# The low part of the attention keys, padded with zero rows to the full height of the matrix array

## The chip, the cores and the metric

One core of a Trainium2 chip runs the kernel. The metric is the device time of one execution in microseconds. Below, PE is TensorE's matrix products, PEld its loads of stationary operands, DVE is VectorE, ACT ScalarE, POOL GpSimd, and SP the engine that issues most DMAs.

## The reference

A single encoder block over 1024 tokens of 1024 channels. A normalised input h goes through one wide projection. Branch A is a bidirectional mLSTM, branch B a neighbourhood attention over a 16 by 64 grid of tokens with 8 heads of 64 channels; the branches are gated, projected, merged and added to the input. The part that the change touches is the score product of branch B:

```
sc = einsum('bhcid,bhacjd->bhciaj', q_blk, k_blk) * scale     # d = 64
sc = where(col_mask, sc + bias, NEG)
p  = softmax(sc)
o  = einsum('bhcin,bhcnd->bhcid', p, v_blk)
```

Everything is float32.

## The kernel before

Every float32 operand x of a matrix product is split in two: hi, which is x rounded to the reduced float32 form of TensorE (float32r), and lo = x - hi. A product is made of hi by hi, hi by lo and lo by hi.

The program runs in stages: the front (normalisation, h transposed, the first projection), then branch B, then the projection of B, then branch A, then the output. The instructions of PE stand in an order written out by hand: `weave` emits a filler, which is a string of dense projections (`dense_cm`, tiles `dps`, 128 rows by 512 columns each), and between its parts the pieces of chains, each piece not before a lag, counted in columns of matrix work, has passed. The other engines' instructions are ordered by the framework's scheduler, except in the front.

In branch B the filler is the projections to v and z, to the merge gates, and to q and k of the next pair of heads; the chain `na_chain` does the attention, one piece after three dense products. The heads are taken in four pairs, the two heads of a pair in the two halves of the 128 partitions. For a pair there are 16 blocks, a block being 128 queries of one head; in all 64. A block consists of

- `na_scores`: two products into one PSUM tile `sps`, then the row maximum (DVE, L766), the exponential (ACT, L768) and the division (DVE, L770, L771), giving `pt`;
- `na_weights`, after the scores of the next block: two or three transposes of `pt` on PE into `tps`, copied to `ptr` as hi and lo;
- `na_values`, two blocks later: products of `ptr` with one stationary tile `vb`, in pairs, into `ops`.

In `na_qk` the PSUM banks of the q and k projection are emptied into three tiles of a pair. `qA[:, hh]` holds a head's 64 rows of hi of q in one half of the partitions and of lo in the other. `kB[:, hh]` holds hi of k in both halves (the second half is a DMA copy). So one product of 128 rows, `qA` by `kB`, gives hi by hi plus lo by hi. `kl` holds lo of k, both heads of a pair in one tile of 128 partitions and 1024 columns, a head in its own half. The second product takes the 64 rows of hi from `qA` and the 64 rows of that head from `kl`. Both products have 384 columns for the inner six blocks of a head and 256 for the two at the edge: 48 and 16 in all.

Of the kernel before, what the change touches and what calls it, by code (L numbers as in the profile page):

```python
# [13 lines left out]
F32R = mybir.dt.float32r  # L14
# [27 lines left out]
def f32(ap):  # L42
    return ap.bitcast(F32)


class Build:
# [3 lines left out]

    # ---------------------------------------------------------------- helpers
    def pool(self, name, bufs=1, **kw):
        return self.tc.tile_pool(name=name, bufs=bufs, reuse_waits="tile", **kw)

    def load_w(self, src, c0, kt0, nk, ncols):
        """Rows kt0*128.. of src, columns as (start, count) parts, to a hi and a lo part."""
        return self.split_w(self.load_raw(src, c0, kt0, nk, ncols), nk, ncols)
# [30 lines left out]
    def weave(self, fill):  # L88
        """Emits fill, whose parts need nothing but loads and splits, and between its parts
        those of the chains, each not before its lag (us of matrix work) has passed.  # L90
        A generator yields a lag, or the name of a flag to wait for."""
        held, alive = None, True
        while True:
            late = None
            for e in self.chains:
                if isinstance(e[0], str):
                    if e[0] not in self.flags:
                        continue
                    e[0] = self.pe
                if late is None or e[0] < late[0]:  # L100
                    late = e
            if held in self.flags:
                held = None
            free = alive and held is None
            if late is not None and (late[0] <= self.pe or not free):
                try:
                    v = next(late[1])
                    late[0] = v if isinstance(v, str) else self.pe + v
                except StopIteration:
                    self.chains.remove(late)  # L110
            elif free:
                try:
                    v = next(fill)
                    held = v if isinstance(v, str) else None
                except StopIteration:
                    alive = False
            else:
                assert not self.chains and not alive, (held, [e[0] for e in self.chains])
                return

    def mm3(self, out, lh, rh, start, stop):
        """(hi + lo).T @ (hi + lo) without lo.T @ lo."""
        self.mm(out, lh[0], rh[0], start, False)
        self.mm(out, lh[0], rh[1], False, False)
        self.mm(out, lh[1], rh[0], False, stop)

    def dense_cm_steps(self, cols, weights, rhs, got):
        """Channel-major: 256 columns against rhs tiles; four banks [ch tile][t half].
        Yields before each half of each k."""
        ncols = sum(n for _, n in cols)  # L130
# [17 lines left out]
    def dense_cm(self, src, cols, rhs, evac, nk=NK, nst=NST):  # L148
        """As dense_cm_steps, each bank in turn over a part's nst rows of tiles."""
        ncols = sum(n for _, n in cols)  # L150
# [16 lines left out]
    def dense_tm(self, src, cols, lhs, evac):  # L167
        """Token-major: 256 columns; bank b holds token tiles 2b and 2b+1."""
        banks = [self.psd.tile([P, 2, 256], F32, name="dps", tag="d") for _ in range(4)]
# [18 lines left out]

    # ---------------------------------------------------------------- constants
    def setup(self):  # L190
# [46 lines left out]

    # ---------------------------------------------------------------- adaLN RMSNorm, h^T
    def front(self, cols):
        """h^T, with the first projection (256 columns) and that of the gates following its tiles."""  # L240
        nc, io = self.nc, self.io
# [229 lines left out]

    # ---------------------------------------------------------------- gate rows of the mLSTM
    def gate_weights(self, raw):
        """Gate columns of w_in as [k, 128]: i forward at 0, i backward at 32, f at 64 and 96;
        of each the four hi parts, then the lo ones."""
        nc, gp = self.nc, self.gwp
# [8 lines left out]
    def gate_rows(self, ps):  # L485
        """Pre-activations, a row per direction and head; the backward ones in reversed time.
        Those of the lo parts of the weights lie four rows on."""
        nc = self.nc
# [82 lines left out]
    def out_gate(self, fp):  # L571
        """Half the residual gate as a row in DRAM."""
        nc, io = self.nc, self.io
# [30 lines left out]

    # ---------------------------------------------------------------- neighbourhood attention
    def na(self, first, gps, ps0, ps1, fill):
        nc, io = self.nc, self.io
        self.yb = [self.ybp.tile([P, T], F32, name=f"yb{p}") for p in range(4)]
        with self.pool("na") as np_:
# [5 lines left out]
            self.ptr = [np_.tile([P, 8, 3, P], F32R, name=f"ptr{a}") for a in range(2)]  # L615
            self.na_pair = {}
            for a in range(2):
                for h in range(2):
                    self.na_qk(0, a, h, first[a])
# [21 lines left out]
    def na_qk(self, pair, a, h, banks):  # L641
        """q as [hi; lo] of each head, k as hi twice and lo; tokens by blocks of 8 columns."""
        nc, np_ = self.nc, self.np_
        if a == 0 and h == 0:
            qA = np_.tile([P, 2, T], F32R, name="qA")
            kB = np_.tile([P, 2, T], F32R, name="kB")
            kl = np_.tile([P, T], F32R, name="kl")
            self.na_pair[pair] = {"qk": (qA, kB, kl)}
        qA, kB, kl = self.na_pair[pair]["qk"]
        src = banks[h].rearrange("p (r c j) -> p r c j", r=8, c=8)  # L650
        for hh in range(2):
            own, oth = slice(hh * 64, hh * 64 + 64), slice(64 - hh * 64, 128 - hh * 64)
            q, k, l = [t.rearrange("p (c r j) -> p r c j", c=8, r=16)[:, h * 8:h * 8 + 8] for t in (qA[:, hh], kB[:, hh], kl)]
            if a == 0:
# [29 lines left out]
    def na_chain(self):  # L684
        """Blocks of 8 columns of queries of each head: scores, then weights, then values."""
        n = 4 * 16
# [48 lines left out]
    def na_head(self, pair, hh):  # L735
        """Tables of 8 * bias + mask, rows of keys beside those of queries."""
        nc, io, np_ = self.nc, self.io, self.np_
# [14 lines left out]
    def na_scores(self, hd, b):  # L752
        nc, np_, hh = self.nc, self.np_, hd["hh"]
        qA, kB, kl = self.na_pair[hd["pair"]]["qk"]
        rows = slice(hh * 64, hh * 64 + 64)
        kbs = [k for k in (b - 1, b, b + 1) if 0 <= k < 8]
# [5 lines left out]
        self.mm(sv, qA[:, hh, qs], kB[:, hh, ks], True, False)  # L762
        self.mm(sv, qA[rows, hh, qs], kl[rows, ks], False, True)
        p_ = np_.tile([P, 384], F32, name="pt", bufs=2)[:, 0:n]
# [51 lines left out]

    # ---------------------------------------------------------------- merge gates, branch B projection
    def gmerge(self, br, g):
        """tanh((g + b) / 2) of 256 channels of branch br, to DRAM."""
        nc, io = self.nc, self.io  # L820
# [32 lines left out]

    # ---------------------------------------------------------------- mLSTM
    def conv(self, mp, banks, ct, out):
        """3-tap convolution over tokens and x * (1 + tanh(x / 2)), which is 2 silu(x)."""
        nc = self.nc
# [70 lines left out]
    def state_step(self, C, kw, v, c, dt, dec, first):  # L928
        """C (fp32, [d, 2, 258]) updated with chunk c."""
        nc = self.nc  # L930
# [104 lines left out]
    def ml_scores(self, mp, c, qh, kh, hd, Pm):  # L1035
        """S^T of chunk c, times the decays of both directions, as hi and lo blocks."""
        nc = self.nc
# [28 lines left out]
    def gated_out(self, mp, hd):  # L1066
        """Output gate, per-head RMSNorm, SiLU gate path; y^T to DRAM."""
        nc, io = self.nc, self.io
# [62 lines left out]
    def branch_a(self):  # L1131
        """Branch A and its projection, whose first products run beside the last of y."""
        nc, io = self.nc, self.io
# [13 lines left out]

    # ---------------------------------------------------------------- merge, output projection, final norm
    def ya_tile(self, k):
# [9 lines left out]
    def proj_a(self, ms, fs):  # L1159
        """Merged branches, in bands of 256 channels; k 6 and 7 hold the last head."""  # L1160
        nc, io = self.nc, self.io
# [65 lines left out]
    def out_tile(self, fp, tt, mhi, mlo, who, wlo, grep, fg):  # L1227
        """128 tokens of the output projection, residual and final RMSNorm."""
        nc, io = self.nc, self.io
# [92 lines left out]
def build(arrays):  # L1322
    nc = bacc.Bacc("TRN2", target_bir_lowering=False, num_devices=1)
    io = {n: nc.dram_tensor("in_" + n, v.shape, mybir.dt.from_np(v.dtype), kind="ExternalInput").ap() for n, v in arrays.items()}
# [11 lines left out]
```

## Time and profile before

| what | value |
|---|---|
| median of 3 runs | 1332.75 us (1330.42 to 1333.08) |
| span of the profiled execution, first to last instruction | 1329.1 us |
| what the median has beyond that span | 3.65 us |
| PE busy | 1305.2 us, 98% of the span |
| DVE, ACT, POOL busy | 49%, 43%, 31% |

The profile is of one execution. The page gives its span and not what lies around it, so the median stands beside the span with 3.65 us more. A busy PE isn't a PE at its peak: matrix products are pipelined, each record is longer than the time from its start to the start of the next, and ends of records are modelled. So the starts are read here, not the ends. The stretch in which the attention blocks lie goes from 86 to 415 us.

### The profile page before, as it was taken

What the parts mean: (1) busy time and instruction counts of PE and PEld (TensorE: products, weight loads), DVE (VectorE), ACT (ScalarE), POOL (GpSimd) and SP (SyncE); (2) the same over time, 40 slices, a digit from 0 to 9 for tenths busy, and PEclk for the clock granted to TensorE, in tenths of its full rate; (3) what the DMA queues carried; (4) which work ended last, traced back from release to release, by engine and by line L of the source; (5) the groups of instructions that cost most, each with busy time, mean ns of one, the idle gap of its engine ahead of it and who ended that gap; (6) DMA issues with size and microseconds to landing.
All of it is one profiled execution on the core that took longest, in us unless ns stands there. A gap on an engine that the chain in (4) does not pass through costs nothing.

```text
span 1329.1 us, 19861 instructions
## 1 busy us (share of the span) xinstructions
PE 1305.2 (98%) x7560; PEld 1127.5 (85%) x7560; DVE 651.8 (49%) x1381; ACT 566.7 (43%) x1191; POOL 418.5 (31%) x381
## 2 busy tenths in 40 slices
PE   8799999999999899999999999999999999999997
PEld 8677777777777688988999989999989989888886
DVE  6944536435345441347626654555625641533533
ACT  6564434334444412336424553364434543423322
POOL 2634434335324423222212222222222212153332
PEclk9999999999999999999999999999999999999999
DMA  9633222222223364112111121112111122446432
GB/s 291 155 88 92 72 61 72 76 56 72 69 66 95 107 208 119 48 41 72 46 42 44 45 73 48 41 44 77 40 40 45 44 80 86 160 136 196 160 101 89
DMA packets 106187, 116.24 MB, mean 87 GB/s; under 512 B 9724, under 2 KB 86012, under 8 KB 106092
## 3 DMA queue, kind: packets, MB, share of 16 engines
q1 hardware_dynamic: 97352, 102.69, 27.1%
q10 hardware_dynamic: 8740, 12.29, 2.7%
q8 instruction: 59, 0.97, 0.3%
q14 instruction: 36, 0.29, 0.1%
HBM read 92.48 MB, written 20.08 MB: 85 GB/s over the span
## 4 chain that ended last, share of the span: by engine, by line
PE 91%; DMA 3%; DVE 2%; SPq 1%; ACT 1%; issue 1%; POOL 0%; ACTq 0%; POOLq 0%; DVEq 0%
PE dps L79 67%; PE ops L79 8%; PE ips L79 5%; PE sps L79 4%; PE cps L79 3%; PE tps L83 1%; PE wps L83 1%; DMA t_d<-gtmp 1%; SPq L251 1%; DMA wor<-in_w_out 1%; DMA wa<-in_w_ada 1%; PE kps L83 0%; PE ytp L83 0%; DVE acc L280 0%; PE gaps L79 0%
## 5 line engine op out<-in xcount | busy, mean ns | idle before, releaser
L74 POOL TENSOR_TENSOR wlo<-wraw,whi 128x512 fp32r<-128x512 f32 x168 | 227.0, 1351 | 585.9 <-ACT whi L73 576.0
L79 PE MATMUL dps<-hhi,whi 128*128 128x512 f32 x768 | 318.7, 415 | 1.0 <-ACT gtmp L827 0.6
L79 PE MATMUL dps<-hhi,wlo 128*128 128x512 f32 x768 | 302.6, 394 | 0.0
L79 PE MATMUL dps<-hlo,whi 128*128 128x512 f32 x768 | 298.8, 392 | 0.0
L79 PE MATMUL dps<-whi,hhi 128*128 128x256 f32 x768 | 217.1, 283 | 0.0
L79 PE MATMUL dps<-wlo,hhi 128*128 128x256 f32 x768 | 217.1, 283 | 0.0
L79 PE MATMUL dps<-whi,hlo 128*128 128x256 f32 x768 | 217.0, 283 | 0.0
L73 ACT ACTIVATE whi<-wraw 128x512 fp32r<-128x512 f32 x168 | 105.6, 629 | 228.6 <-PE dps L79 186.5
L79 PEld LDWEIGHTS dps<-hhi,whi 128*128 128x128 f32 x768 | 145.3, 189 | 32.2 <-issue 10.6
L79 PEld LDWEIGHTS dps<-hhi,wlo 128*128 128x128 f32 x768 | 145.2, 189 | 32.3
L79 PEld LDWEIGHTS dps<-hlo,whi 128*128 128x128 f32 x768 | 145.3, 189 | 18.6 <-DVE hlo L342 0.4
L79 PEld LDWEIGHTS dps<-wlo,hhi 128*128 128x128 f32 x768 | 146.9, 191 | 0.2
L79 PEld LDWEIGHTS dps<-whi,hhi 128*128 128x128 f32 x768 | 146.9, 191 | 0.2
L79 PEld LDWEIGHTS dps<-whi,hlo 128*128 128x128 f32 x768 | 146.9, 191 | 0.0
L79 PE MATMUL dps<-ya,whi 128*128 128x512 f32 x256 | 79.3, 391 | 0.0
L768 ACT ACTIVATE pt<-pt,mx 128x384 f32<-128x384 f32 (+1 forms) x64 | 37.7, 589 | 94.6 <-DVE mx L766 94.2
L1052 POOL TENSOR_TENSOR dg<-negm,mmask 128x256 f32<-128x256 f32 x32 | 25.0, 781 | 98.7 <-issue 28.9
L79 PEld LDWEIGHTS dps<-ya,whi 128*128 128x128 f32 x256 | 47.6, 188 | 9.7 <-DVE t0r L1182 0.2
L79 PE MATMUL ops<-woh,mlo 128*128 128x512 f32 (+1 forms) x136 | 51.3, 377 | 0.0
L79 PE MATMUL ops<-wol,mhi 128*128 128x512 f32 (+1 forms) x136 | 51.2, 377 | 0.0
L79 PE MATMUL ops<-woh,mhi 128*128 128x512 f32 (+1 forms) x136 | 51.2, 377 | 0.0
L79 PE MATMUL dps<-ya,wlo 128*128 128x512 f32 x128 | 49.9, 389 | 0.0
(265 smaller groups left out, 2359.1 us busy)
## 6 DMA issues: line engine op xcount, KB each, us to landing
wraw<-in_w_in SPq DMA_DIRECT2D x112, 256.0 KB
wa<-in_w_ada SPq DMA_DIRECT2D x16, 512.0 KB
wraw<-in_w_in SPq DMA_DIRECT2D x64, 128.0 KB
t_d<-gtmp ACTq DMA_DIRECT2D x32, 256.0 KB
xt<-in_x SPq DMA_DIRECT2D x8, 512.0 KB
wag<-in_w_ada SPq DMA_DIRECT2D x16, 256.0 KB
t1r<-t_d SPq DMA_DIRECT2D x8, 512.0 KB
mp_d<-t1r SPq DMA_DIRECT2D x16, 256.0 KB
```

Source lines behind the costliest of these rows:

```text
L73: nc.scalar.activation(hi, raw, AF.Copy)
L74: nc.gpsimd.tensor_tensor(lo, raw, f32(hi), op=ALU.subtract)
L79: self.nc.tensor.matmul(out, lhsT=lhsT, rhs=rhs, start=start, stop=stop, skip_group_check=True)
L83: self.nc.tensor.transpose(out, src, ident)
L251: nc.sync.dma_start(wa[:, :, s, :], wv[:, :, s, k, :])
L768: nc.scalar.activation(p_, p_, AF.Exp, bias=mx, scale=-1.0, accum_out=sm)
L1052: nc.gpsimd.tensor_tensor(dg, negm.rearrange("p (a b) -> p a b", a=2), mk, op=ALU.add)
```

## The change

`kl` becomes one tile of 128 partitions, two heads and 1024 columns, made once for all pairs. For each head the half of the partitions that isn't its own is set to zero once, by two GpSimd memsets of 64 rows by 1024 columns each, ahead of the first `na_qk`. The head's lo of k goes to its own half as before. The second score product takes all 128 rows of `qA[:, hh]` and of `kl[:, hh]`: the rows of lo of q meet zeros. It has the same stationary operand as the first one. In the build, the memory set aside per partition for dynamic DMA descriptors is given as 1024 bytes. All else in the diff is comments and docstrings that became blank lines.

```diff
+            self.kl = np_.tile([P, 2, T], F32R, name="kl")
+            for hh in range(2):
+                nc.gpsimd.memset(f32(self.kl)[64 - hh * 64:128 - hh * 64, hh], 0.0)
             for a in range(2):
                 for h in range(2):
                     self.na_qk(0, a, h, first[a])
...
-            kl = np_.tile([P, T], F32R, name="kl")
-            self.na_pair[pair] = {"qk": (qA, kB, kl)}
+            self.na_pair[pair] = {"qk": (qA, kB, self.kl)}
...
-            q, k, l = [t.rearrange("p (c r j) -> p c r j", c=8, r=16)[:, h * 8:h * 8 + 8] for t in (qA[:, hh], kB[:, hh], kl)]
+            q, k, l = [t.rearrange("p (c r j) -> p c r j", c=8, r=16)[:, h * 8:h * 8 + 8] for t in (qA[:, hh], kB[:, hh], kl[:, hh])]
...
-        rows = slice(hh * 64, hh * 64 + 64)
...
         self.mm(sv, qA[:, hh, qs], kB[:, hh, ks], True, False)
-        self.mm(sv, qA[rows, hh, qs], kl[rows, ks], False, True)
+        self.mm(sv, qA[:, hh, qs], kl[:, hh, ks], False, True)
...
-    nc = bacc.Bacc("TRN2", target_bir_lowering=False, num_devices=1)
+    nc = bacc.Bacc("TRN2", target_bir_lowering=False, num_devices=1, dynamic_dma_scratch_size=1024)
```

## Rows read from the trace of the kernel before

**Rows 1.** The page: span, and the chain that ended last by engine.
```profile
span 1329.1 us, 19861 instructions
...
PE 91%; DMA 3%; DVE 2%; SPq 1%; ACT 1%; issue 1%; POOL 0%; ACTq 0%; POOLq 0%; DVEq 0%
```

**Rows 2.** One stretch: us, busy us of PE PEld DVE ACT POOL, granted clock, DMA.
```profile
170.00:260.00 90.00, 89.90 (x417) 69.74 (x417) 42.55 (x106) 38.10 (x85) 33.14 (x25) 1.00 0.26 71
```

**Rows 3.** Groups of PE's instructions by shape: count, busy us, mean ns, idle before.
```profile
L79 PE MATMUL sps<-kl,qA 64*128 64x384 f32 x48 | 21.0, 437 | 0.0
...
L79 PE MATMUL sps<-kB,qA 128*128 128x384 f32 x48 | 16.3, 339 | 0.0
...
L79 PE MATMUL sps<-kl,qA 64*128 64x256 f32 x16 | 6.1, 380 | 0.0
...
L79 PE MATMUL sps<-kB,qA 128*128 128x256 f32 x16 | 4.4, 276 | 0.0
```

**Rows 4.** Timeline of one block: start us, duration us, engine, instruction.
```profile
200.32 0.34 PE L79 MATMUL sps<-kB,qA 128*128 128x384 f32 x1
200.59 0.18 PEld L79 LDWEIGHTS sps<-kl,qA 64*128 64x128 f32 x1 [0.31 <-issue]
200.59 0.44 PE L79 MATMUL sps<-kl,qA 64*128 64x384 f32 x1
...
200.96 0.50 PE L79 MATMUL dps<-hhi,whi 128*128 128x512 f32 x1
...
201.29 0.39 PE L79 MATMUL dps<-hlo,whi 128*128 128x512 f32 x1
...
202.55 0.42 PEld L79 LDWEIGHTS ops<-ptr,vb 128*128 128x128 f32 x2
...
202.78 0.51 PE L79 MATMUL ops<-ptr,vb 128*128 128x384 f32 x2
...
203.13 0.40 PE L79 MATMUL dps<-hhi,whi 128*128 128x512 f32 x1
...
203.38 0.39 PE L79 MATMUL dps<-hlo,whi 128*128 128x512 f32 x1
```

**Rows 5.** The chain in order of time, near 111 us: start, us, what.
```profile
110.25 0.35 PE ops L79 x2
110.60 0.70 PE dps L79 x3
111.30 0.55 PE sps L79 x2
111.84 0.89 PE dps L79 x3
```

**Rows 6.** Timeline of PE at 458 us, transposes of 36 rows.
```profile
458.14 0.39 PE L79 MATMUL dps<-ybhi,wlo 128*128 128x512 f32 x1
458.46 0.68 PE L83 MATMUL gps<-ident,nat 36*128 36x36 f32 x8
459.07 0.51 PE L79 MATMUL dps<-ybhi,whi 128*128 128x512 f32 x1
459.41 0.40 PE L79 MATMUL dps<-yblo,whi 128*128 128x512 f32 x1
```

**Rows 7.** Timeline of POOL at the start of branch B.
```profile
70.53 0.95 POOL L491 MEMSET li<- 40x1024 f32 x1
73.41 0.95 POOL L492 MEMSET lz<- 40x1024 f32 x1 [1.94 <-PE gaps L79]
```

**Rows 8.** Timeline: last write of kl for pair 0, and PE taking that bank.
```profile
76.20 0.69 DVE L659 TENSOR_TENSOR kl<-dps,kB 64x512 fp32r<-64x512 f32 x1 [0.63 <-ACT kB L658]
...
77.29 0.39 PE L79 MATMUL dps<-hhi,whi 128*128 128x512 f32 x1
```

**Rows 9.** Timeline: the block whose weights are ready latest.
```profile
88.12 0.71 DVE L771 TENSOR_SCALAR pt<-pt,rc 128x256 f32<-128x256 f32 x1
...
88.89 0.44 PE L83 MATMUL tps<-ident,pt 128*128 128x128 f32 x2
```

More of the change, by code (lines that the diff above doesn't have):

```diff
@@ L652, in na_qk @@
             own, oth = slice(hh * 64, hh * 64 + 64), slice(64 - hh * 64, 128 - hh * 64)
-            q, k, l = [t.rearrange("p (c r j) -> p r c j", c=8, r=16)[:, h * 8:h * 8 + 8] for t in (qA[:, hh], kB[:, hh], kl)]
+            q, k, l = [t.rearrange("p (c r j) -> p r c j", c=8, r=16)[:, h * 8:h * 8 + 8] for t in (qA[:, hh], kB[:, hh], kl[:, hh])]
             if a == 0:
```

## The prediction

> **What bounds the kernel now.** I first read the page's chain that ended last: PE holds 91% of it, and DMA, the next, 3% [rows 1]. So a time taken out of PE counts, if it is taken where PE leads. Second, the sums by stretch, for branch B. In the 90 us shown PE is busy 89.90 at the full granted clock, 1.00 of 2.4 GHz, while DVE has 42.55, ACT 38.10 and POOL 33.14 [rows 2]; the three other stretches that I asked for between 90 and 420 us look the same. PE has practically no gap there and no other engine is more than half full. So in this stage the time is the sum of the distances from the start of one matrix product to the start of the next.
>
> Third, the groups by shape. The first score product, 128 rows by 384 columns, has a mean of 339 ns, the second, 64 rows by the same 384 columns, 437; with 256 columns it is 276 and 380 [rows 3]. The half-height product is the longer one, by 98 and 104 ns, so the excess doesn't go by columns. Since ends of PE records are modelled, I go by starts, in the timeline of one block [rows 4]. The reader is to see three things there. The first score product starts at 200.32, the second at 200.59, the dense product behind them at 200.96, and the next dense product only at 201.29: 0.97 us for two products of 384 columns and one of 512. The weight load of the second score product starts at 200.59, the very moment at which its product is put, with 0.31 us of idle before it: it was not done ahead. And 2 us later the same sequence stands with 128 rows throughout: two products `ops` of 384 columns with one stationary tile between them, start 202.78, then dense products at 203.13 and 203.38, which is 0.60 us. Their two loads lie from 202.55 to 202.97, beside the products.
>
> **The change part by part.**
>
> *The second score product gets 128 rows.* It streams the same columns, so what changes is the surplus. For a block of 384 columns the timeline gives 0.97 - 0.60 = 0.37 us [rows 4]. The chain in order of time, which counts by ends, gives (0.55 + 0.89) for the score pair and its three dense products against (0.35 + 0.70) for the pair `ops` and its three: 0.39 us [rows 5]. For the 16 blocks of 256 columns the surplus of the records is the same within 6 ns (98 against 104, [rows 3]), so I price all 64 alike: 64 x 0.37 = 23.7 us at the low end, 64 x 0.39 = 25.0 us at the high end. I take 0.38, 24.3 us.
>
> Where the surplus sits: an `ops` product takes (203.13 - 202.78) / 2 = 0.175 us from start to start, the first score product 0.27 and the second 0.37; a dense product takes 0.70 / 3 = 0.23, the one behind the pair 0.33 [rows 4, 5]. So it is 0.1 us on going down to 64 rows, 0.2 on coming back up, and 0.1 on the product after. That this belongs to a change of height and not to these tiles is seen at another place. Eight transposes of 36 rows stand between dense products; the product before them starts at 458.14 and they at 458.46, 0.32 us instead of 0.23, and behind them 459.07 to 459.41 is 0.34 us [rows 6]: the same 0.1 on the way down and on the product after. After the change no score block changes height.
>
> So the rows show a time that depends on the height, the lower product being dearer, by 0.1 us on the record [rows 3] and 0.37 us on the sequence [rows 4]. A rule of the Trainium skill speaks against the change here: TensorE: Matmul & The Clock Gate, table under "Why this matters for your kernels", says that a single product of 32 rows takes as long as one of 128, and by it this edit would be worth 0 instead of 24.3 us. This trace doesn't agree with it where heights are mixed in one sequence.
>
> *One stationary tile for both products.* The number of loads doesn't change: PE and PEld have one load per product throughout, also where two neighbours share a tile, as `ops` does (x2 loads, x2 products, [rows 4]). So I count nothing for a load left out. The load becomes 128 rows high; it hides beside the first product, as that of the second `ops` product does. If that cover were gone, it would be the rival below.
>
> *Two memsets on POOL.* A memset of 40 rows by 1024 columns takes 0.95 us [rows 7]; with the same columns the two take 1.9 us, once. They can go after the last work of the front, where POOL has done the memset of `li` by 71.48 and then waits 1.94 us for PE [rows 7]; this hides them. If they are not hidden, what is behind them on POOL is the memset of `lz` and then the lo parts of weights, and the cost is at most their 1.9 us. If the write of `kl` by DVE were also made to wait for them, DVE's writes of pair 0 would end later: the last one ends at 76.20 + 0.69 = 76.89 and PE takes its bank at 77.29, a slack of 0.40 us [rows 8], so a wait for the whole 1.9 us would cost PE 1.5 us. Bounds 0 to 1.9 us; near the low end, since the idle time just there covers them, I take 0.3.
>
> *The tile `kl` made once.* Before, it has one buffer, so the next pair's writes waited for this pair's reads; they still do, and `qA` and `kB`, which stay as they were, have the same wait. 0. The smaller descriptor memory: no instruction of the kernel issues a DMA from GpSimd, and `POOLq` has 0% of the chain [rows 1]. 0 from both sides as far as the rows go.
>
> *What is late next.* PE reaches the transposes of a block about 0.4 us earlier after its scores. In the tightest block the weights are ready at 88.12 + 0.71 = 88.83 and the transposes start at 88.89 [rows 9]: PE waits there already, and this block gives its share back. Of the 64 blocks three more have under 0.3 us between, all others over 0.5, mostly about 2. I take 4 x 0.2 = 0.8 us given back; bounds 0 to 4 x 0.38 = 1.5.
>
> Sum: 24.3 - 0.3 - 0.8 = 23.2 us, bounds 23.7 - 1.9 - 1.5 = 20.3 and 25.0. The profiled execution's span would go from 1329.1 to 1305.9. What lies around it I leave at the 3.65 us between span and median, so the median goes from 1332.75 to 1309.5. With the spread of the runs before (2.3 us below the median, 0.3 above) the likeliest case alone has 1305 to 1313.
>
> **The rivals.**
>
> *Part of the gain is given back all through branch B* (the softmax between ACT and DVE, or the splits of weights by ACT and POOL, become the bound). Against it: DVE at 42.55 of 90 us would be at 42.55 of about 84 [rows 2]. For it: the order on those engines is the scheduler's and may come out differently. If half is lost, 12 us of gain: 1320.7.
>
> *Nothing changes.* The surplus would belong to the place (two products into one small bank behind dense work) and not to the height. Against it: `ops` also writes one bank twice [rows 4], and the 36-row transposes, at another place, show the same 0.1 us steps [rows 6]. Time 1332.75, or up to 1.9 more with the memsets not hidden. The rule of equal time for all heights, cited above, ends here too.
>
> *Slower: the second load of the same rows isn't overlapped.* Both products now use all the rows, and the load of the second could be held until the first is through, and the dense load until the second is. Then from the first score product on: 0.34 + 0.18 + 0.34 + 0.18 = 1.04 us, with the product of 0.34 and the load of 0.18 us of [rows 4], and then the dense product at the usual 0.23: 1.27 against 0.97, or 0.30 x 64 = 19.2 us more, 1352. It decides for slower by over 0.2% from 2.7 / 64 = 0.04 us on, so a sequence of over 1.01 us. TensorE: Matmul & The Clock Gate, Part 3, "What overlaps and what doesn't", says that a load overlaps products in flight only when its group of rows differs, which would be this case. The rows don't bear it out: the loads of 128 rows for `ops` lie beside products of 128 rows, and the load that is not done ahead is the one of 64 rows [rows 4].
>
> **How the numbers follow.** Likeliest, the full gain: 0.84, 1309.5 us. Half of it given back: 0.08. Nothing: 0.05. Slower: 0.03. 0.2% is 2.7 us, about what a measurement of this kernel can tell from no change. So faster 0.92, same 0.05, slower 0.03. The range 1304 to 1318 takes in the whole of the likeliest case with its unknown costs and the smaller part of the give-back case; that is a little over 8 in 10.
>
> **What would show it.** The profile after should have for both products of `sps` groups of 128 rows with a mean near 339, where the second now has 437; in the timeline of a block some 0.60 us from the first score product to the second dense product behind it, with both score loads done ahead and no idle time "issue" before them; branch B shorter by 23 to 25 us; and the stages behind unchanged in length. The prediction is wrong if the pair keeps 0.9 us or more, if PE shows gaps in branch B that wait for DVE, ACT or POOL, or if the front ends later by more than the two memsets.

## The result, and the profile after

The kernel after takes 1315.46 us in the median of 4 runs (1314.33 to 1316.92), the kernel before 1331.88 (1330.42 to 1333.08, 4 runs). The ratio is 0.9875, with a 95% interval of 0.9861 to 0.9889: 16.4 us or 1.25% faster. That is within the range of 1304 to 1318 us, and 6.0 us above the forecast of 1309.5. So the kind and the place of the gain came as said; the size of one term did not. The 1315.46 us lie above the 1305 to 1313 that the likeliest case alone had.

The profiled execution took 1316.2 us, 1.8 of it around its span. The page of the kernel after, span and chain by engine, answers to [rows 1]:

```profile
span 1314.4 us, 19862 instructions
...
PE 88%; DVE 6%; DMA 2%; issue 2%; ACT 1%; POOL 0%; SPq 0%; ACTq 0%; POOLq 0%; DVEq 0%
```

DVE now has 6% of the chain where it had 2%: something waits for DVE that did not before. The groups by shape of the kernel after, which answer to [rows 3]:

```profile
L79 PE MATMUL sps<-kl,qA 128*128 128x384 f32 x48 | 16.2, 338 | 0.0
L79 PE MATMUL sps<-kl,qA 128*128 128x256 f32 x16 | 4.5, 282 | 0.0
L79 PE MATMUL sps<-kB,qA 128*128 128x256 f32 x16 | 4.4, 277 | 0.0
```

The second score product now has the duration of the first: 338 ns where it had 437, with the same columns; the first is unchanged at 339. In the timeline of one block of the kernel after the reader is to see the starts, as in [rows 4]:

```profile
196.00 0.34 PE L79 MATMUL sps<-kB,qA 128*128 128x384 f32 x1
196.17 0.34 PE L79 MATMUL sps<-kl,qA 128*128 128x384 f32 x1
196.17 0.19 PEld L79 LDWEIGHTS dps<-hhi,whi 128*128 128x128 f32 x1
196.34 0.40 PE L79 MATMUL dps<-hhi,whi 128*128 128x512 f32 x1
196.58 0.39 PE L79 MATMUL dps<-hlo,whi 128*128 128x512 f32 x1
```

From the first score product to the second dense product behind it are 0.58 us, where it was 0.97. As a median over all blocks this distance is 586 ns for the 48 with 384 columns (972 before) and 466 ns for the 16 with 256 (853 before). The surplus that is gone is 48 x 0.386 + 16 x 0.387 = 24.7 us. The dense load lies beside the second score product, and nothing stands idle before it.

But the stretch does not end 24.7 us earlier. The busy time by stretch, from the first score product to the first product of the projection of B, and from there to the end, first for the kernel before (us, then busy us of PE, PEld, DVE, ACT and POOL, granted clock, DMA):

```profile
86.13:456.87 370.74, 367.72 (x1693) 283.89 (x1691) 180.35 (x426) 160.98 (x348) 149.74 (x112) 1.00 0.26 74
456.87:1329.13 872.26, 861.42 (x5464) 778.69 (x5464) 410.98 (x834) 351.93 (x752) 226.23 (x224) 1.00 0.28 82
```

and for the kernel after, with a 90 us stretch that answers to [rows 2]:

```profile
86.14:440.09 353.95, 345.05 (x1692) 284.83 (x1690) 182.31 (x426) 159.19 (x349) 149.60 (x112) 1.00 0.27 78
440.09:1314.41 874.32, 863.79 (x5464) 781.01 (x5464) 410.69 (x834) 351.75 (x752) 226.98 (x224) 0.99 0.27 82
...
164.00:254.00 90.00, 88.50 (x439) 73.74 (x439) 43.40 (x110) 39.02 (x88) 34.45 (x26) 1.00 0.28 76
```

The front is as long as it was (86.13 and 86.14). Branch B is shorter by 370.74 - 353.95 = 16.8 us, with a granted clock of 1.00 in both. PE had 370.74 - 367.72 = 3.0 us without work in it and now has 8.9. What lies behind is longer by 2.1 us. In the waits of PE of the kernel after (us, times, longest) four groups are new that the waits of before do not have at all. One, 0.5 us of `dps` for `hhi`, stands in the front; that of `ops` stands in the output stage:

```profile
PE tps L83 <- DVE ptr L786: 5.3, 5, 1.4
...
PE ops L79 <- DVE t0r L1183: 1.5, 1, 1.5
PE tps L83 <- DVE pt L772: 0.9, 1, 0.9
```

`tps` are the transposes of `na_weights`. Counted by starts (from the dense product ahead to the transposes, less the usual 0.23 us), 12 of the 64 sets are late, by 7.9 us together; before it was 0.1, so 7.8 us are new. 24.7 - 7.8 = 16.9, which is the 16.8 of branch B within 0.1. Two smaller terms by starts nearly cancel: 0.6 us more between the transposes of one block, 0.4 less between dense products.

One such place in full, in the timeline of the kernel after:

```profile
122.32 1.30 POOL L74 TENSOR_TENSOR wlo<-wraw,whi 128x512 fp32r<-128x512 f32 x1
122.50 2.83 DVE L772 TENSOR_SCALAR pt<-pt,rc 128x256 f32<-128x256 f32 x1
123.58 1.59 POOL L584 TENSOR_SCALAR gacc<-wag,cs 128x512 f32<-128x512 f32 x1
123.90 0.40 PE L79 MATMUL dps<-hhi,wlo 128*128 128x512 f32 x1
125.13 1.61 POOL L586 TENSOR_SCALAR wag<-wag,cs 128x512 f32<-128x512 f32 x1
125.24 0.41 DVE L786 TENSOR_TENSOR ptr<-tps,ptr 128x256 fp32r<-128x256 f32 x1
125.71 0.44 PE L83 MATMUL tps<-ident,pt 128*128 128x128 f32 x2 [1.41 <-DVE ptr L786]
```

and the same place in the kernel before:

```profile
123.78 1.30 POOL L74 TENSOR_TENSOR wlo<-wraw,whi 128x512 fp32r<-128x512 f32 x1
124.42 0.80 DVE L771 TENSOR_SCALAR pt<-pt,rc 128x256 f32<-128x256 f32 x1
...
125.05 1.61 POOL L584 TENSOR_SCALAR gacc<-wag,cs 128x512 f32<-128x512 f32 x1
...
125.14 0.41 DVE L785 TENSOR_TENSOR ptr<-tps,ptr 128x256 fp32r<-128x256 f32 x1
126.45 0.38 PE L83 MATMUL tps<-ident,pt 128*128 128x128 f32 x2
```

Read it from the last line of the first fence backwards. The transposes wait 1.41 us for the copy that empties the one `tps` bank of the block before. The copy stands in DVE's order behind the division of the next block. This division took 2.83 us, although the median of all 64 is 0.42: it began in one GpSimd instruction, `wlo`, and ended as the one after it, `gacc`, did (123.58 + 1.59 = 125.17). In the kernel before `gacc` follows `wlo` just as closely, but the division began 0.64 us into `wlo` and ended 0.14 us behind it (125.22 to 125.08), not with `gacc` (126.66); the copy was done at 125.55 and the transposes came at 126.45, 0.9 us later. The order of the instructions on each engine is the same in the two kernels, but for the two new memsets; only the times at which the engines meet have shifted. The same happens at 207.7 and 292.5 us, with divisions of 2.8 us. These three places make 4.7 of the 7.9 us. At 390.0 us it is different: that division takes 2.25 us, but it was held through two GpSimd instructions in the kernel before as well, as its timeline shows:

```profile
405.81 2.23 DVE L771 TENSOR_SCALAR pt<-pt,rc 128x384 f32<-128x384 f32 x1
```

There the transposes were 0.13 us late, and now they are 1.0 late. So at this place the hold is not new, and only the wait behind it grew. Another 1.0 us is the first block, whose transposes wait for the division itself; the other seven sets have 1.2 us together.

### The profile page after: what moved, and what is told of

Its sections match the earlier page's. It is cut to its first block, busy times and chain, and to the rows that moved or that the text cites. A ratio compares the mean times of both kernels' runs of the same rounds, so it can differ in the third digit from the quotient of the medians.

```text
span 1314.4 us, 19862 instructions
## 1 busy us (share of the span) xinstructions
PE 1283.4 (98%) x7560; PEld 1128.7 (86%) x7560; DVE 652.2 (50%) x1381; ACT 564.6 (43%) x1191; POOL 420.4 (32%) x383
## 4 chain that ended last, share of the span: by engine, by line
PE 88%; DVE 6%; DMA 2%; issue 2%; ACT 1%; POOL 0%; SPq 0%; ACTq 0%; POOLq 0%; DVEq 0%
PE dps L79 65%; PE ops L79 8%; PE ips L79 5%; PE sps L79 3%; PE cps L79 3%; DVE acc L280 2%; PE tps L83 2%; DVE pt L772 1%; DMA wa<-in_w_ada 1%; PE kps L83 0%; PE ytp L83 0%; PE wps L83 0%; DMA wor<-in_w_out 0%; PE gaps L79 0%; DMA t_d<-gtmp 0%
## 5 line engine op out<-in xcount | busy, mean ns | idle before, releaser
L79 PE MATMUL dps<-hhi,whi 128*128 128x512 f32 x768 | 311.2, 405 | 1.2 <-ACT hhi L338 0.5
```

What stands on the lines that cost most here:

```text
L79: self.nc.tensor.matmul(out, lhsT=lhsT, rhs=rhs, start=start, stop=stop, skip_group_check=True)
```

## The experiments

Theory, on the gain: the height of the product is what costs, and the change takes away 0.39 us in each of 64 blocks. Theory, on what is given back: copies held on DVE behind a division that GpSimd holds. Rivals: the gain comes of the shared stationary tile; the loss comes of the division itself being awaited, of GpSimd's work as such, or of other parts of the change.

**e1: 128 rows, but another stationary tile.** The second product takes the tile of the other head, so that its scores are of wrong data.

```diff
-        self.mm(sv, qA[:, hh, qs], kl[:, hh, ks], False, True)
+        self.mm(sv, qA[:, 1 - hh, qs], kl[:, hh, ks], False, True)
```

> The changed kernel, but the second score product takes its stationary tile from the other head of the pair, so the two products no longer share one (the scores then come out wrong; the work, its shapes and its order stay). Theory (only the change of height costs): from start to start the pair keeps 0.17 and 0.17 us and the dense product behind it 0.23, and the time stays that of the changed kernel, 1315 us within 3. Rival (the shared stationary tile saves a load or lets it go ahead): the pair and the dense product behind go up by up to 0.39 us per block, up to 24.6 us over 64 blocks, towards 1332.

1314.82 us (1313.69 to 1315.32), ratio 0.9872 (0.9857 to 0.9887): that of the change itself. The ends of a block in its timeline:

```profile
195.67 0.34 PE L79 MATMUL sps<-kB,qA 128*128 128x384 f32 x1
...
196.25 0.39 PE L79 MATMUL dps<-hlo,whi 128*128 128x512 f32 x1
```

0.58 us again. That the two products share one stationary tile buys nothing; the height does it.

**e2: 128 rows for one head of each pair.** Half the dose: the other head keeps its 64 rows.

```diff
+        if hh == 0:
+            self.mm(sv, qA[:, hh, qs], kl[:, hh, ks], False, True)
+        else:
+            self.mm(sv, qA[64:128, hh, qs], kl[64:128, hh, ks], False, True)
```

> The changed kernel with the second score product at 128 rows only for the first head of each pair; the second head takes its 64 rows as before. Theory: the 32 blocks of the first head take 0.58 us from the first score product to the second dense product behind (0.47 with 256 columns), the other 32 take 0.97 (0.85); matrix work falls by 32 x 0.385 = 12.3 us, half of the whole, so 1319.6 us plus whatever waits appear. If the waits for the copies of the transposed weights (7.9 us in the changed kernel) come from the shorter distance between blocks, they shrink to less than half, 1320 to 1323; if they come from something else in the edit, they stay and it is near 1327.

1319.69 us (1316.70 to 1319.93), ratio 0.9902 (0.9886 to 0.9919), so about 12 of the 16 us with half the change. The changed blocks took 586 and 468 ns in the median, the others 976 and 855, and the transposes waited 1.0 us in all. Half the surplus, 12.3 us, less 1.0 is 11.3. The first half of the dose is nearly free of the loss; 6.9 of the 7.9 us come with the second. The three divisions of 2.8 us are not there: the one over 2 us, 2.23, is that of the kernel before.

**e3 and e4: the price of a change of height.** In the kernel before each score product is cut into two halves of its columns. In e3 the heights run 128, 128, 64, 64; in e4 128, 64, 128, 64. The same instructions, and one more way down and up in e4.

```diff
+        order = ((0, 0), (0, 1), (1, 0), (1, 1))   # e3; e4: ((0, 0), (1, 0), (0, 1), (1, 1))
+        for t, (kind, part) in enumerate(order):
...
+            if kind:
+                self.mm(sv[:, x:y], qA[rows, hh, qs], kl[rows, cols], False, t == 3)
+            else:
+                self.mm(sv[:, x:y], qA[:, hh, qs], kB[:, hh, cols], t == 0, False)
```

> The kernel before with each score product cut into two of half the columns, in the order 128, 128, 64, 64 rows: still one way down and one way up per block. Theory: the surplus of 0.385 us per block is still paid once; the cut itself adds what two more products cost. Products of 128 columns stand 0.11 us apart in the kernel before, so a block of 256 columns goes from 2 x 0.12 to 4 x 0.11 (+0.2) and one of 384 from 2 x 0.175 to about 4 x 0.11 (+0.09): 48 x 0.09 + 16 x 0.2 = 7.5 us more than before, 1339 us within 4. Rival (the surplus belongs to each product of 64 rows): twice the surplus, 25 us more, 1364.

> The same four products per block as in the run with two cut products in a row, in the order 128, 64, 128, 64 rows: two ways down and two up per block. Theory (each way down and up costs about half a surplus of 0.385 us): 64 x 0.385 = 24.6 us more than the run with the order 128, 128, 64, 64, within 6. Rival (the surplus belongs to the products of 64 rows or to the place): the same time as that run within 3.

One run each: 1335.82 and 1356.15 us, 20.3 us apart. A block of e3:

```profile
201.63 0.36 PE L79 MATMUL sps<-kB,qA 128*128 128x192 f32 x2
201.93 0.46 PE L79 MATMUL sps<-kl,qA 64*128 64x192 f32 x2
202.32 0.50 PE L79 MATMUL dps<-hhi,whi 128*128 128x512 f32 x1
202.66 0.40 PE L79 MATMUL dps<-hlo,whi 128*128 128x512 f32 x1
```

and of e4:

```profile
208.54 0.25 PE L79 MATMUL sps<-kB,qA 128*128 128x192 f32 x1
208.72 0.35 PE L79 MATMUL sps<-kl,qA 64*128 64x192 f32 x1
...
209.57 0.50 PE L79 MATMUL dps<-hhi,whi 128*128 128x512 f32 x1
209.91 0.39 PE L79 MATMUL dps<-hlo,whi 128*128 128x512 f32 x1
```

1.03 us against 1.37; in the median over all blocks 1023 and 1366 ns with 384 columns, 966 and 1252 with 256. The further way down and up costs 0.34 and 0.29 us, 48 x 0.343 + 16 x 0.286 = 21.0 us in all, near the 20.3 of the times. In e3 two low products in a row pay once. This is the sign that the change of height, and not the low product as such, costs. These runs and the change itself put 0.29 to 0.39 us on each way down and up. The Trainium skill, TensorEngine Tiling (Array Packing), Key Properties, says that a change of the tiling mode drains the engine; no run here shows whether a product of 64 rows among products of 128 is such a change.

e4 also says something of the loss. Its blocks are longer than those of the kernel before, and yet two of its sets of transposes are 1.0 us late each, behind divisions like this one:

```profile
223.41 3.03 DVE L780 TENSOR_SCALAR pt<-pt,rc 128x256 f32<-128x256 f32 x1
```

So shorter blocks are not needed for such a wait; other times at which the engines meet are enough.

**e8: all of the change but the rows.** The tile for both heads, the memsets and the smaller descriptor memory stay; the product takes 64 rows.

```diff
-        self.mm(sv, qA[:, hh, qs], kl[:, hh, ks], False, True)
+        self.mm(sv, qA[rows, hh, qs], kl[rows, hh, ks], False, True)
```

> The changed kernel with its tile for both heads, its memsets and its smaller descriptor memory, but with the second score product at 64 rows as in the kernel before. Theory (only the height of the product matters): the time of the kernel before, 1331.9 within 2, with the pair and what follows at 0.97 us per block and no new waits. Rival (the other parts cost or gain something): over 2 us from 1331.9, and then this explains as much of the 8 us that are missing in the result.

1331.48 us (10 runs), ratio 0.9997 (0.9988 to 1.0006): no change, and the product is the long one again, with the 437 ns of [rows 3].

**e5: the division on ACT.** By the theory GpSimd does not hold it there.

```diff
-        nc.vector.tensor_scalar_mul(p_, p_, rc)
+        nc.scalar.activation(p_, p_, AF.Copy, scale=rc)
```

> The changed kernel with the division of the weights (64 instructions on VectorE, 0.42 us each where alone, up to 2.83 us beside work of GpSimd) done by ScalarE. Theory (the 7.9 us of new waits of the transposes come from copies of the weights queued on VectorE behind a division that is held up while GpSimd works): the waits of over 0.5 us go, matrix work in branch B has no gap over 0.5 us, and the time falls by 5 to 7 us, from 1315 to about 1309. Rival (the distance between blocks is now too short for the whole round of reduction, exponential, division, transposes and copies, with one bank for the transposes): moving the division to ScalarE, which already does the exponential and one of the two copies, doesn't shorten the round; waits stay at 6 us or more and the time within 2 us of 1315.

1312.02 us (1310.33 to 1313.13), ratio 0.9847 (0.9834 to 0.9860): 3.4 us below the kernel after, where 5 to 7 were expected. The transposes still waited 5.5 us, 2.4 less than in the kernel after, though no division took over 0.62 us on ACT. PE's waits of e5 have many short ones in place of the few long:

```profile
PE tps L83 <- DVE ptr L786: 3.8, 8, 0.5
```

and the timeline of e5 says for what:

```profile
128.96 0.56 DVE L767 CUSTOM_DVE_ANT_0 pt<-sps,tint 128x384 f32<-128x384 f32 x1 [1.50 <-PE sps L79]
129.44 0.55 DVE L786 TENSOR_TENSOR ptr<-tps,ptr 128x384 fp32r<-128x384 f32 x1
130.14 0.41 PE L83 MATMUL tps<-ident,pt 128*128 128x128 f32 x2 [0.52 <-DVE ptr L786]
```

With the division gone, the copy stands on DVE behind the maximum of the next block's scores, which itself waits for PE. So the division was one thing that can stand ahead of the copy, not the only one.

**e6: the division made to come after the copy.** An extra instruction of one column makes the division of a block depend on the copy of the block before, and it is issued behind `na_weights`.

```diff
+        nc.vector.scalar_tensor_tensor(sm, self.last_lo, 0.0, sm, op0=ALU.mult, op1=ALU.add)
         nc.vector.reciprocal(rc, sm)
         nc.vector.tensor_scalar_mul(p_, p_, rc)
...
         nc.vector.tensor_tensor(dst[1], tp[:, i0:i0 + n, :], f32(dst[0]), op=ALU.subtract)
+        self.last_lo = f32(flat[1])[:, start, 0:1]
```

> The changed kernel with the division of a block put behind the copy of the previous block's transposed weights on VectorE, by making it depend on that copy (one more instruction of one column per block); it stays on VectorE. Theory (the copy is late only because it is queued behind a held-up division): divisions of over 2 us remain in the trace, but the copy no longer stands behind them; the four waits of 1.2 to 1.8 us go, 5 to 6.5 us in all, to about 1309.5. Rival (the round is too short as a whole): the waits stay, or move to the transposes waiting for the division, and the time is 1315 within 2 or higher.

1336.83 us (1334.55 to 1338.63), ratio 1.0030 (1.0017 to 1.0042): slower than the kernel before. The theory's way to mend it fell. PE's waits of e6:

```profile
PE tps L83 <- DVE pt L783: 21.4, 23, 3.0
```

The transposes no longer wait for the copy but for the division, and 26 us in all. The two inputs of the transposes, a free bank and a divided block, both lie on DVE; putting one off for the other moves the wait.

**e7: fewer GpSimd instructions.** Of the sums for the output gate only the first product of each is left, so the gate is that of part of its input.

```diff
-                else:
-                    nc.gpsimd.tensor_scalar_mul(wa, wa, c)
-                    nc.gpsimd.tensor_tensor(acc[:, h], acc[:, h], wa, op=ALU.add)
```

> The changed kernel without 14 of the 16 pairs of GpSimd instructions that weigh and sum rows for the residual gate beside branch B (the gate is then wrong; their loads stay). Theory (a division is held up where two or more GpSimd instructions follow each other without a gap): divisions of 2.2 to 2.8 us fall below 1.7 us, and the waits of 1.2 us and more at them, four in all, go where they were caused by these sums (391 us, and those of 124, 209 and 294 us whose second GpSimd instruction is one of these sums), 3 to 5.5 us, to about 1311. Rival (GpSimd has no part in it): the divisions and the waits stay as they are, 1315 within 2.

1311.18 us (1310.88 to 1313.38), ratio 0.9845 (0.9832 to 0.9859). The waits of the transposes at 209, 294 and 391 us are gone, and those at 124, where the kept instruction stands, stay. The first of the places that are gone, in the timeline of e7:

```profile
207.62 1.29 POOL L74 TENSOR_TENSOR wlo<-wraw,whi 128x512 fp32r<-128x512 f32 x1
207.78 1.28 DVE L769 TENSOR_SCALAR pt<-pt,rc 128x256 f32<-128x256 f32 x1
```

The division begins 0.16 us into `wlo`, where it began 0.18 us into it in the kernel after, and with no second GpSimd instruction behind `wlo` it takes 1.28 us, not 2.82. But 5.5 us of waits are left, because new ones appear at 134, 218 and 302 us, one of them:

```profile
132.13 1.28 POOL L812 TENSOR_TENSOR yb<-osum,zz 64x512 f32<-64x512 f32 x1 [7.36 <-DVE osum L811]
132.43 2.45 DVE L769 TENSOR_SCALAR pt<-pt,rc 128x384 f32<-128x384 f32 x1
133.37 1.29 POOL L74 TENSOR_TENSOR wlo<-wraw,whi 128x512 fp32r<-128x512 f32 x1
```

Again two GpSimd instructions without a gap (132.13 + 1.28 = 133.41), and a division that begins in the first and ends with the second (134.66 and 134.88). So it need not be the gate's work; other instructions that stand back to back do it too. They do not always: of the 13 divisions of the kernel after that begin in a GpSimd instruction with another less than 0.1 us behind it, 4 were held through the second and 9 were not; in the kernel before it was 1 of 12. What decides, no run shows.

**e9: the division in another form.** A scalar_tensor_tensor that multiplies by 1/sum and by a tile of ones; the order on DVE stays but for one pair of neighbours.

```diff
-        nc.vector.tensor_scalar_mul(p_, p_, rc)
+        nc.vector.scalar_tensor_tensor(p_, p_, rc, self.one3[:, 0:n], op0=ALU.mult, op1=ALU.mult)
```

> The changed kernel with the division of the weights in another form on VectorE: weights times reciprocal times a tile of ones, two tensor operands instead of one, in the same place of the same order. Theory (the form with one tensor operand is what is held up while GpSimd works; a form that isn't leaves no copy late): no division over 1.2 us, the waits of the transposes for copies fall from 7.9 us to under 3, and the time from 1315 to 1309 or 1311. Rival 1 (any VectorE instruction on these tiles is held up by GpSimd): divisions of 2 us and more remain and the time is 1315 within 2. Rival 2 (the round is too short as a whole): divisions shrink, the waits and the time don't.

1311.71 us (1310.70 to 1312.07), ratio 0.9846 (0.9833 to 0.9860); the transposes waited 4.1 us, where under 3 were expected. The place of the stall at 122.5 us, and one at the end, in the timeline of e9:

```profile
122.81 1.59 DVE L774 SCALAR_TENSOR_TENSOR pt<-pt,rc,one 128x256 f32<-128x256 f32 x1
124.05 1.78 POOL L584 TENSOR_SCALAR gacc<-wag,cs 128x512 f32<-128x512 f32 x1
...
386.39 2.44 DVE L774 SCALAR_TENSOR_TENSOR pt<-pt,rc,one 128x384 f32<-128x384 f32 x1
```

The division is dearer when nothing disturbs it (median 620 against 421 ns). At 122.8 us it was held through one GpSimd instruction, `wlo`, and ended 0.35 us into `gacc`; at 386.4 us it was held through two all the same, and its transposes were 1.2 us late. Ten divisions took over 1.2 us, where none was expected to. So this form is held up too. Since a longer division also moves all that follows, e9 does not show whether the form or the times took the three long holds away.

**e10, e11 and e12: the values ahead of the transposes.** The lists of a step of `na_chain` change places on PE, so that a block's transposes come three dense products later. e10 is the kernel after with this, e11 has e9's division as well, and e12 is the kernel before with this order alone.

```diff
-            if 1 <= i <= n:
-                self.na_weights(heads[(i - 1) // 8], (i - 1) % 8)
-                yield NLAG
...
                 self.na_values(heads[j // 8], j % 8)
                 if j % 16 == 15:
                     self.flags.add(f"na{pair}")
                 yield NLAG
+            if 1 <= i <= n:
+                self.na_weights(heads[(i - 1) // 8], (i - 1) % 8)
+                yield NLAG
```

> The changed kernel with the products of the values emitted ahead of the transposes of the weights in every block, which puts one value product pair and three dense products, about 1.05 us, more between a block's division and the next transposes; the divisions stay held up. Theory (the wait is what is left of a late copy after the slack): the waits of 1.2 to 1.8 us fall by about 1 us each and those under 0.7 vanish, 7.9 us to about 3, time 1310 to 1311. Rival (the waits follow the divisions wherever the transposes stand): 1315 within 2.

> Both edits: the division with two tensor operands and the values ahead of the transposes. Theory: no wait of the transposes over 0.3 us, matrix work in branch B without gaps, the whole surplus of 24.6 us kept: span 1329.1 - 24.6 = 1304.5 within 2, time 1306 to 1309. Rival (something else also gives gain back): waits of over 2 us in all remain, 1311 or more.

> The kernel before, with 64 rows in the second score product, and only the products of the values put ahead of the transposes, as in the run that did so on the changed kernel (1310.2 us). Theory (the held-up divisions cost matrix time only because the padded product shortens the distance between blocks): nothing to gain, since the transposes wait 0.13 us in all before; 1332 within 2. Rival (the order is better in itself by the 5 us seen there): 1327.

| kernel | median us | ratio to the kernel before, 95% | transposes waited, us |
|---|---|---|---|
| after | 1315.46 | 0.9875 (0.9861 to 0.9889) | 7.9 |
| e10 | 1310.16 (1308.91 to 1312.91) | 0.9842 (0.9828 to 0.9855) | 1.0 |
| e11 | 1309.73 (1308.76 to 1313.91) | 0.9839 (0.9822 to 0.9855) | 1.0 |
| e12 | 1332.96 (1331.19 to 1334.71) | 1.0007 (0.9999 to 1.0016) | 0.0 |

e10 and e11 are the fastest seen, e11 not in the 1306 to 1309 us expected of it. They are not told apart, nor are e5, e7 and e9 by their intervals. On the kernel before the order is worth nothing, on the kernel after some 5 us: it buys back waits that the kernel before did not have. But it does not do so by the later place alone. The divisions were expected to stay held up in e10; the divisions by duration (shortest, median, longest, in ns) show that they did not:

```profile
L772 DVE TENSOR_SCALAR pt<-pt,rc x64: 354/422/1305, 87.8 to 396.5; 128x384 f32<-128x384 f32 x48, 128x256 f32<-128x256 f32 x16
```

The longest is 1.31 us, against 2.83 in the kernel after. The median time from a copy to the next transposes grew from 1.12 to 1.52 us. e10 changes both, and no run tells what each is worth. The stretch of branch B took 350.3 us in e10 and 349.5 in e11, 20.4 and 21.2 below the kernel before; in e5 and e9 it took 350.0 and 350.1. Of the 24.7 us the transposes still cost 1.0, in the first blocks; and PE's waits of e10 have a new row of the values, which now come sooner behind their copies:

```profile
PE ops L79 <- DVE ptr L786: 1.8, 4, 0.8
```

24.7 - 1.0 - 1.8 = 21.9 against 20.4: some 1.5 us in e10, and 0.7 by the same sum in e11, were not traced. The stretch differs by as much with no change in the blocks: in e8 it took 369.3 us, against 370.7. Of the 5 us, 3.6 lie in branch B (354.0 to 350.3), the rest behind it.

## Why the prediction was right, and where it was off

*The second product at 128 rows* was taken at 0.38 us a block, 24.3 in all, from the sequence in [rows 4] and [rows 5]. It measured 0.386, 24.7. The reading of starts and not of durations was what made this right: the records alone fell by 437 - 338 = 99 ns [rows 3], a quarter of it. e3 and e4 show the price with the same instructions in another order, at 0.29 to 0.34 us.

*One stationary tile*: counted at nothing, and nothing by e1.

*Memsets*: 0.3 us taken, none found. POOL at the start of branch B in the kernel after:

```profile
70.65 1.95 POOL L619 MEMSET kl<- 64x1024 f32 x2
...
73.45 0.95 POOL L492 MEMSET lz<- 40x1024 f32 x1
```

They lie where POOL idled, and `lz` begins at 73.45 where it began at 73.41 [rows 7]. e8 has them, with the tile and the descriptor memory, at a ratio of 0.9997.

*"What is late next"* is the step that failed: 0.8 us taken, 1.5 as its bound, 7.8 measured, in a mechanism of the right kind (PE reaches the transposes sooner). Two things must be ready for the transposes, the divided block and the free `tps` bank. The step read the first, division to transposes, for all blocks, and never the second, copy to transposes. In 60 of 63 blocks of the kernel before the second had the less time to spare, 1.70 us in the median against 2.12. It also took 0.38 us as the most that a block could lose. In most blocks that nothing disturbed, the time to spare behind the copy fell by 0.57 to 0.60 us (1.12 in the median of all blocks): 0.2 and 0.1 us of the block's own surplus lie behind the start of its second score product and 0.39 us of the next block's pair come before the transposes, less 0.11 us by which DVE can begin on the scores sooner. And the slack is not fixed: with blocks of another length the division meets other GpSimd instructions. At 122 us it was 2.83 us long where it had been 0.80, and the 0.9 us of slack became a wait of 1.41. That the copy's place on DVE and the division held by GpSimd make this wait is shown by the two timelines, and by e5 and e7, which each change one of them and move or shorten the waits. That the waits go when the transposes come later, e10 shows, but not that the later place alone does it. Which block will be hit, no run lets one say ahead.

*The sum of branch B*: 23.2 forecast, 16.8 measured. The loss in full, against the span: 23.2 - 14.7 = 8.5 us, which is 7.0 of the transposes and 2.1 of the later stages, less 0.4 of the surplus and 0.3 of the memsets, within 0.1. Of the 2.1, 1.5 are the wait for `t0r` at the first output product. There DVE stood 1.68 us for ACT's `woh`. This wait differs by kernel (0 before, 0.4 in e9, 0 in e10) though nothing near it was changed; its cause stays open.

*The base* was off the other way. Around the span lie 1.8 us in the kernel after, and 1.9 in another run of the kernel before (1331.99 us with a span of 1330.1), not 3.65: the profiled execution of before stood some 1.8 us below the median of its three runs. With that of after standing 0.7 above its own median, 8.5 - (3.65 - 1.8) - 0.7 = 5.9 is the 6.0 us by which the median was missed.

*The range and the signs.* The span became 14.7 us shorter, which lies below the sum's own bounds of 20.3 to 25.0. The time lies in the range because the range was made wider for a partial give-back; that the base was 1.85 us too high, which made up for part of the missed loss, was luck. Of the prediction's signs, those on the second product came true (338 ns, 0.58 us, no idle time before the loads). Three did not: PE has gaps in branch B that wait for DVE, which was to show the prediction wrong; branch B is shorter by 16.8 us and not by 23 to 25; and the stages behind are 2.1 us longer.

*The rivals.* "Given back through branch B" was priced at half; a third came (7.8 of 24.7), so the truth lies between it and the likeliest case. "Nothing changes" and "the second load isn't overlapped" fall with the timeline of a block: 0.58 us, and two score products 0.17 us apart by their starts, less than the 0.19 us of a load, so that the second's load must lie beside the first. The rule of the Trainium skill that the prediction cites for the last (TensorE: Matmul & The Clock Gate, Part 3), that loads overlap products only where the group of rows differs, does not hold in this trace.

## What to carry to other kernels

In a sequence that PE bounds, look at starts and keep one height of matrix product: padding with zero rows cost nothing here beyond two hidden memsets, and saved 0.39 us for each way down and up. When such a stretch gets shorter, read for each PE instruction every thing that it waits for, the release of its PSUM bank too, and look at what is queued ahead of that release on its engine; the slack of before does not bound the loss, since the engines meet at other times. Then try the instruction a step later: here that was worth nothing before the change and some 5 us after it, though it moved the long holds away as well.

## Seen of the hardware, not expected

A VectorE instruction from SBUF to SBUF, 0.42 us in the median, took up to 2.83 us in the kernel after beside GpSimd, and 3.03 in e4. Where it was held, it mostly ended 0.15 to 0.22 us behind the GpSimd instruction that it began in. Some were held to the end of the next when the two stood back to back, most were not. With a second tile as input it was held through two once, for 2.44 us. The Trainium skill, SBUF — State Buffer, section "Who interferes with whom", says that a VectorE instruction in a mode that takes two ports, which a `tensor_scalar` can enter, and GpSimd share a pair of ports under an exclusive lock, and that the other blocks fully until the one that issued first has finished. The trace agrees with it at 207.8 us in e7, where the division ended 0.15 us behind `wlo`. It does not everywhere: in the kernel before a division that began at 127.40 us, 0.76 us into `wag` of GpSimd, took its usual 0.42 us and was over 0.47 us before it.

Two products of 64 rows in a row in e3 pay for the change of height once, not for each. So do, as far as one place shows it, eight transposes of 36 rows [rows 6]: from the start of the first, 458.46 us, to that of the product behind them, 459.07, is 0.61 us, 0.08 for each.
